# Letting a timeline-based scheduler order the instructions of a two-layer diffusion-step kernel

## The chip, the cores and the metric

The kernel runs on one core of a Trainium2 chip. The metric is the device time of one execution in microseconds (us). A core has five engines that run side by side, each working through its own list of instructions in order: PE (TensorE, matmuls), DVE (VectorE), ACT (ScalarE), POOL (GpSimd) and SP (SyncE, which here only starts DMA transfers). Engines wait for each other by semaphores. So the time depends not only on what is computed but also on the order in which each engine's list is written.

## The reference

One inference step of a hybrid backbone with two layers, on 128 prompt tokens and 512 latent tokens. Both go through the same weights, each modulated by its own condition. Layer 0 mixes tokens by latent attention (MLA) and neighbourhood attention, layer 1 by grouped-query attention. Each is followed by a SwiGLU feed-forward network (FFN), and a final norm ends the step. Cut to what matters here:

```python
def swiglu(h, w_in, w_out):
    gate, up = jnp.split(h @ w_in, 2, axis=-1)
    return (jax.nn.silu(gate) * up) @ w_out
...
    for l in range(DEPTH):
        ...
        xs = xs + g1_s * out_s
        hp = modulate(rms_norm(xp, norm_ffn[l]), sh2_p, sc2_p)
        hs = modulate(rms_norm(xs, norm_ffn[l]), sh2_s, sc2_s)
        xp = xp + g2_p * swiglu(hp, w_ffn_in[l], w_ffn_out[l])
        xs = xs + g2_s * swiglu(hs, w_ffn_in[l], w_ffn_out[l])
```

## The kernel before

**Layout.** All 640 tokens lie along the free axis, the 1024 features on the partitions in 8 tiles `xr`. The tokens are halved, so a matmul works on 128 x 128 weights and 320 tokens. Each float32 operand is split into a high part and a low remainder (`h` and `l` at the end of a name), which TensorE takes as fp32r. A product then is three matmuls per 128 x 128 tile (`mm3`, line 188): high by high, high by low, low by high. ACT makes the high part with a copy, DVE the low part with a subtraction, for weights (`unit`, line 175) and for activations (`rsplit`, line 456).

**Stages.** Input projections and attention of layer 0, output projection and residual (`mixer_out`, line 1115, tiles `oa0a` to `oa7b`, weights `oaw0` to `oaw7`), FFN (`ffn`, line 1214), then the same for layer 1 (tiles `oc`), and the final norm. Side work is mixed in: the modulation vectors of layer 1 are formed by passes on DVE over weights `wm` (tile `junk`, line 1796).

**The FFN's first half.** The 2816 hidden features are 22 blocks. Blocks 0 and 1 are done with plain products (`eight`). Blocks 2 to 21 use seven products over half the reduction and half the tokens in place of eight. Per block `n` these are: 11 (bank `fg`, weights `wX`), D (bank `fd`, `wY`), N (into `fg`, `wZ`), 21 (bank `fu`, `wX`), 22 (into `fd`, `wZ`), C (into `fg`, `wY`) and E (into `fg`, `wW`). Each is 12 matmuls. Between them banks are read out: ACT copies `fg` after product 11 to `p`, `fd` after D, `fg` after N to `u`; DVE forms `up` from `fu` and `fd`, and after C it forms `g<-fg,p`, which ACT's Silu turns into half of `sg`. E then adds into the same bank `fg` and gives the other half. In the code E of a block is issued in the loop's next pass:

```python
            after(PE.last, lambda: product(b5, w.Y, 0, "D", True))
            act(S.activation, p5, b5[:, :HT], AF.Copy)
...
                jb, jg, jW, jup, jsg = job
                product(jg, jW, 0, "E", False)
...
            product(g, w.Y, 512, "C", False)
            dve(V.tensor_tensor, g2, g[:, :HT], p5, ALU.add)
            act(S.activation, sg[:, HT:T], g2, AF.Silu, scale=-1.0)
            job, w = (fb, g, w.W, up, sg), n
```

DVE and ACT instructions of this loop go through `Line` (line 1233), which pins each behind the one before on its engine. PE's products aren't pinned there, except D. The hidden tiles are `hd` (kept) or are spilled to memory and read back as `hr`.

**The FFN's second half.** Tiles `fo` add up products of hidden tiles with weights `wo`, which are loaded, split and used one after another (`wout`). The residual (line 319) adds the result to `xr` on DVE.

**What sets the order.** The program names operations in one sequence. The framework's scheduler (`tile.TileContext`, line 2249) turns this into one list per engine, with the semaphores that data and buffers need. It may move an operation as long as its inputs, its buffers and the pins (`issue_after`, used by `after`, `run` and `Line`) allow. The pools (`bufs=`) decide how far loads can run ahead.

## Time and profile before

| | |
|---|---|
| median of 3 runs | 1482.27 us (1481.26 to 1484.97) |
| the profiled execution's own time (its span) | 1482.4 us |
| instructions in the profile | 25722 |
| read from memory, written | 192.23 MB, 34.69 MB |
| DMA transfers started by SP (queue q1) | 219.73 MB, 43.3% of 16 engines' span |

A row of the profile gives the start, the duration, the engine, the source line (L63 is PE's matmul helper, L1239 the `Line` helper, so names of tiles tell the rows apart), the operation, output and inputs, shape and count. In square brackets stands how long the engine was idle before, and what released it. Some other rows give a group's times as min/median/max ns. The names leave out the numbers of blocks and layers: `fg<-h01E,wW` is product E of any block in layer 0, `fg<-h11E,wW` of layer 1.

### The profile page before, as it was taken

How to read it: one execution, taken by the hardware profiler on the slowest of the kernel's cores; microseconds unless marked ns; L12 is line 12 of the kernel's file. 1: busy time of each engine (PE TensorE's matmuls, PEld its weight loads, DVE VectorE, ACT ScalarE, POOL GpSimd, SP SyncE). 2: the span in 40 equal slices, each digit the busy share in tenths (PEclk: the TensorE clock that was granted, in tenths of full speed). 3: DMA queues.
4: the chain of work that ended last, by engine and by line, in shares of the span. 5: the costliest groups of instructions: out<-in, count | busy, mean ns of one | idle time of the engine just before them, and what ended most of it. 6: DMA issues, size and time to landing. Idle time of an engine off the chain costs nothing.

```text
span 1482.4 us, 25722 instructions
## 1 busy us (share of the span) xinstructions
PE 1443.7 (97%) x9785; PEld 1394.3 (94%) x9785; DVE 1210.9 (82%) x2278; ACT 772.0 (52%) x1525; POOL 207.0 (14%) x298
## 2 busy tenths in 40 slices
PE   5999989999999999999999999999999999999997
PEld 4988978889999999999999999989999999999996
DVE  5786788886999999977997888775899999954496
ACT  5445677873755444441123666663755555542253
POOL 0226534432000000000001322222000000000000
PEclk9999999999999999999999999999999999999998
DMA  9644511016055555569763211004055556668522
GB/s 368 223 146 138 181 39 43 30 32 211 29 196 171 187 185 183 185 211 344 275 209 128 86 55 46 29 31 135 30 186 177 184 192 206 212 224 308 194 87 72
DMA packets 79900, 228.61 MB, mean 154 GB/s; under 512 B 8864, under 2 KB 14272, under 8 KB 79392
## 3 DMA queue, kind: packets, MB, share of 16 engines
q1 hardware_dynamic: 76832, 219.73, 43.3%
q0 software_dynamic: 1600, 5.14, 1.0%
q10 hardware_dynamic: 1344, 2.10, 0.4%
q8 instruction: 77, 1.26, 0.3%
q14 instruction: 47, 0.39, 0.1%
HBM read 192.23 MB, written 34.69 MB: 153 GB/s over the span
## 4 chain that ended last, share of the span: by engine, by line
PE 83%; DVE 7%; ACT 5%; DMA 2%; issue 2%; POOL 0%; DVEq 0%; ACTq 0%; SPq 0%; POOLq 0%
PE fg L63 21%; PE fd L63 9%; PE fo L63 8%; PE fu L63 6%; PE gq L63 3%; PE nq L63 2%; PE nk L63 2%; PE fo_2b L63 1%; PE fo_0b L63 1%; PE gs L63 1%; PE fo_2a L63 1%; PE fo_0a L63 1%; PE go L63 1%; PE mod L63 1%; PE fo_4b L63 1%
## 5 line engine op out<-in xcount | busy, mean ns | idle before, releaser
L1796 DVE SCALAR_TENSOR_TENSOR junk<-wm,cb 128x1024 bf16<-128x1024 f32 x62 | 75.6, 1220 | 4.6 <-DMA wm<-in_wm 4.1
L1239 ACT ACTIVATE sg<-g 128x320 f32<-128x320 f32 x34 | 16.0, 472 | 114.9 <-DVE g L1239 114.9
L63 PE MATMUL gq<-h10h,wgq 128*128 128x320 f32 x256 | 66.7, 318 | 0.0
L255 POOL TENSOR_SCALAR h10h<-h10t,gs,mods 128x320 fp32r<-128x320 f32 x4 | 3.6, 890 | 429.4 <-DVE h10t L249 427.7
L1239 DVE SCALAR_TENSOR_TENSOR junk<-wm,cb 128x1024 bf16<-128x1024 f32 x50 | 61.0, 1221 | 0.8
L1239 DVE TENSOR_TENSOR wY<-s,wY 128x1024 fp32r<-128x1024 f32 x40 | 48.8, 1220 | 1.1 <-ACT wY L1239 1.0
L1239 DVE TENSOR_TENSOR wZ<-s,wZ 128x1024 fp32r<-128x1024 f32 x40 | 48.8, 1220 | 0.0
L63 PEld LDWEIGHTS gq<-h10h,wgq 128*128 128x128 f32 x256 | 45.0, 188 | 0.9 <-PE gtp L67 0.2
L1239 ACT ACTIVATE wZ<-s 128x1024 fp32r<-128x1024 f32 x40 | 42.4, 1060 | 0.1
L1239 ACT ACTIVATE wY<-s 128x1024 fp32r<-128x1024 f32 x40 | 42.0, 1049 | 0.0
L63 PE MATMUL gq<-h10l,wgq 128*128 128x320 f32 x128 | 39.5, 308 | 0.0
L1978 ACT ACTIVATE gp<-gs,gb,rq 128x640 f32<-128x640 f32 (+1 forms) x40 | 31.9, 797 | 14.5 <-DVE gb L1977 14.1
L63 PE MATMUL fg<-h11E,wW 128*128 128x320 f32 x240 | 38.7, 310 | 0.0
L63 PE MATMUL fg<-h01q,wX 128*128 128x320 f32 x240 | 38.6, 309 | 0.0
L63 PE MATMUL fg<-h11q,wX 128*128 128x320 f32 x240 | 38.6, 309 | 0.0
L63 PE MATMUL fg<-h01N,wZ 128*128 128x320 f32 x240 | 38.6, 309 | 0.0
L63 PE MATMUL fg<-h11N,wZ 128*128 128x320 f32 x240 | 38.6, 309 | 0.0
L63 PE MATMUL fu<-h01q,wX 128*128 128x320 f32 x240 | 38.6, 308 | 0.0
L63 PE MATMUL fu<-h11q,wX 128*128 128x320 f32 x240 | 38.6, 309 | 0.0
L63 PE MATMUL fg<-h01E,wW 128*128 128x320 f32 x240 | 38.6, 309 | 0.0
L63 PE MATMUL fd<-h01q,wZ 128*128 128x320 f32 x240 | 38.5, 309 | 0.0
L63 PE MATMUL fd<-h11q,wZ 128*128 128x320 f32 x240 | 38.5, 309 | 0.0
(3226 smaller groups left out, 5249.6 us busy)
## 6 DMA issues: line engine op xcount, KB each, us to landing
wm<-in_wm SPq DMA_DIRECT2D x48, 512.0 KB, 3.6
mraw<-in_wm SPq DMA_DIRECT2D x8, 1024.0 KB, 15.4
mraw<-in_wm SPq DMA_DIRECT2D x16, 512.0 KB, 3.9
hr_T<-sp_T SPq DMA_DIRECT2D x21, 320.0 KB, 5.9
hr_B<-sp_B SPq DMA_DIRECT2D x18, 320.0 KB, 6.1
mrow<-in_wm0g POOLq DMA_DIRECT2D x8, 512.0 KB, 6.2
wm<-in_wm0g SPq DMA_DIRECT2D x8, 512.0 KB, 3.4
x<-in_xT SPq DMA_DIRECT2D x8, 320.0 KB, 5.7
```

The costliest lines, as they stand in the source:

```text
L63: cls.last = nc.tensor.matmul(*a, **k)
L255: G.tensor_scalar(h[:, c0:c1], t, self.gsl[:, k, 0:1], self.ml[:, self.sh + k, 0:1], ALU.mult, ALU.add)
L1239: self.last = after(self.last, lambda: op(*a, **k))
L1796: def step(kind, at, line=lambda op, *a, **k: op(*a, **k)):
L1978: weighed.append((S.activation(dst, src, AF.Exp, bias=nb, scale=rq[:, j:j + 1], accum_out=ll[:, j:j + 1]), v))
```

## The change

One argument: the scheduler no longer finds the order by its default rule but with a simulation of the engines' timelines.

```diff
     for name, shape in _OUTS:
         args.append(nc.dram_tensor(f"out_{name}", shape, F32, kind="ExternalOutput").ap())
-    with tile.TileContext(nc) as tc:
+    with tile.TileContext(nc, schedule_with_timeline_sim=True) as tc:
         body(tc, *args)
```

The instructions are the same in both kernels, engine by engine; only their order differs, and with it the semaphore waits and some buffers' turns. PE's list changes most in the FFN loops of both layers (up to 82 places), around the output projections (up to 75) and in the FFN's second half (up to 88). It is the same in the stretch from 111 to 296 us of the profile. DVE's and ACT's lists are the same inside the FFN loops and differ by small moves elsewhere. The three places that the prediction rests on follow; in them a name's last number only tells tiles of one name apart.

*PE in the FFN loop of layer 0.* `fg_8` is the bank of block 8. Before, between product C and product E of block 8 (`h01C`, `h01E`):

```order
L63 MATMUL fg_8_6073<-h01C_4787,wY_8_5934 128x320 x3
L63 MATMUL fg_8_6073<-h01C_4788,wY_8_5934 128x320 x3
L63 MATMUL fg_9_6209<-h01q_4765,wX_9_6069 128x320 x3
L63 MATMUL fg_9_6209<-h01q_4766,wX_9_6069 128x320 x3
L63 MATMUL fg_9_6209<-h01q_4767,wX_9_6069 128x320 x3
L63 MATMUL fg_9_6209<-h01q_4768,wX_9_6069 128x320 x3
L63 MATMUL fd_9_6193<-h01D_4781,wY_9_6070 128x320 x3
L63 MATMUL fd_9_6193<-h01D_4782,wY_9_6070 128x320 x3
L63 MATMUL fd_9_6193<-h01D_4783,wY_9_6070 128x320 x3
L63 MATMUL fd_9_6193<-h01D_4784,wY_9_6070 128x320 x3
L63 MATMUL fg_8_6073<-h01E_4793,wW_8_5987 128x320 x3
```

Now at the same place of PE's list:

```order
L63 MATMUL fd_9_6193<-h01D_4784,wY_9_6070 128x320 x3
L63 MATMUL fg_8_6073<-h01C_4785,wY_8_5934 128x320 x3
L63 MATMUL fg_8_6073<-h01C_4786,wY_8_5934 128x320 x3
L63 MATMUL fg_8_6073<-h01C_4787,wY_8_5934 128x320 x3
L63 MATMUL fg_8_6073<-h01C_4788,wY_8_5934 128x320 x3
L63 MATMUL fg_8_6073<-h01E_4793,wW_8_5987 128x320 x3
L63 MATMUL fg_8_6073<-h01E_4794,wW_8_5987 128x320 x3
L63 MATMUL fg_8_6073<-h01E_4795,wW_8_5987 128x320 x3
L63 MATMUL fg_8_6073<-h01E_4796,wW_8_5987 128x320 x3
L63 MATMUL fg_10_6345<-h01q_4765,wX_10_6205 128x320 x2
L63 MATMUL fu_10_6346<-h01q_4769,wX_10_6205 128x320 x2
L63 MATMUL fg_9_6209<-h01N_4789,wZ_9_6071 128x320 x3
```

Product D of block 9 and product 11 of block 9 have moved ahead of C of block 8, so E follows C with nothing between; two matmuls each of products 11 and 21 of block 10 come behind E.

*PE where the attention of layer 0 ends.* `mo` and `mpp3o` are the last attention values, `oMs3` is their split, `oa` the output projection. Now PE's list has:

```order
L63 MATMUL mo_4223<-mts_4l,mv_2867 128x512
L63 MATMUL mpp3o<-mpp3pth,mv_2851 128x128
L63 MATMUL mpp3o<-mpp3ptl,mv_2851 128x128
L63 MATMUL mpp3o<-mpp3pth,mv_2851 128x128
L63 MATMUL mpp3o<-mpp3ptl,mv_2851 128x128
L63 MATMUL oa0a<-oMs3h,oaw_3439 128x320
L63 MATMUL oa0b<-oMs3h,oaw_3439 128x320
L63 MATMUL oa1a<-oMs3h,oaw_4331 128x320
L63 MATMUL oa1b<-oMs3h,oaw_4331 128x320
L63 MATMUL oa2a<-oMs3h,oaw_4412 128x320
L63 MATMUL oa0a<-oMs3l,oaw_3439 128x320
```

Before, 45 matmuls into `oa0b`, `oa1a` and `oa1b` stood between `mpp3o` and the first `oMs3h`; they and 21 matmuls into `oa2a` have moved ahead of the last values.

*DVE behind that place.* `xr_4379` and `xr_4393` are tiles 0 and 1 of the residual, `oaw_4546` is the weight tile oaw4. Before:

```order
L1822 COPY xr_4716<-oMs3l 128x1
L323 SCALAR_TENSOR_TENSOR xr_4379<-oa0a,mods_98,xr_4379 128x320
L323 SCALAR_TENSOR_TENSOR xr_4379<-oa0b,mods_98,xr_4379 128x192
L323 SCALAR_TENSOR_TENSOR xr_4379<-oa0b,mods_98,xr_4379 128x128
L323 SCALAR_TENSOR_TENSOR xr_4393<-oa1a,mods_98,xr_4393 128x320
L323 SCALAR_TENSOR_TENSOR xr_4393<-oa1b,mods_98,xr_4393 128x192
L323 SCALAR_TENSOR_TENSOR xr_4393<-oa1b,mods_98,xr_4393 128x128
L185 TENSOR_TENSOR oaw_4546<-oaw4r,oaw_4546 128x1024
```

Now:

```order
L1822 COPY xr_4716<-oMs3l 128x1
L185 TENSOR_TENSOR oaw_4546<-oaw4r,oaw_4546 128x1024
L323 SCALAR_TENSOR_TENSOR xr_4379<-oa0a,mods_98,xr_4379 128x320
L323 SCALAR_TENSOR_TENSOR xr_4379<-oa0b,mods_98,xr_4379 128x192
L323 SCALAR_TENSOR_TENSOR xr_4379<-oa0b,mods_98,xr_4379 128x128
```

The low part of oaw4 has moved ahead of the residual of tile 0.

Where the FFN loops end, `hd_0` (the last block's hidden tile) is needed by PE six matmuls after the last product E; before, 39 output matmuls stood there. On ACT in layer 0 the split of `wo_13` has moved ahead of `hd_0h`, and on DVE three passes over `wm` stand ahead of the last `sg`. On SP the reads of spilled tiles `hr` have moved ahead of the loads `wo_45` (layer 0) and `wo_26`, `wo_36` and `wo_45` (layer 1).

## The prediction, made before the changed kernel ran

> **What bounds the kernel now.** I read the page's busy line and the engine shares of the chain of waits first: how full TensorE is decides whether an order can win or only lose.

> ```profile
> PE 1443.7 (97%) x9785; PEld 1394.3 (94%) x9785; DVE 1210.9 (82%) x2278; ACT 772.0 (52%) x1525; POOL 207.0 (14%) x298
> PE 83%; DVE 7%; ACT 5%; DMA 2%; issue 2%; POOL 0%; DVEq 0%; ACTq 0%; SPq 0%; POOLq 0%
> ```

> The profiled execution has a span of 1482.4 us and nothing around it, and the median of the runs is 1482.27, so I count from 1482.4. TensorE (PE) is not busy for 1482.4 − 1443.7 = 38.7 us. That is all that any new order could gain. Next the view by stretches of time (width, then busy us of PE, weight loads, VectorE, ScalarE and GpSimd, the granted clock, the DMA share, GB/s) shows where these holes are.

> ```profile
> 185.00:296.00 111.00, 102.97 (x641) 91.50 (x641) 96.43 (x230) 87.92 (x210) 47.77 (x67) 0.98 0.11 37
> 296.00:345.00 49.00, 47.08 (x311) 43.13 (x310) 36.48 (x77) 30.71 (x63) 14.57 (x15) 1.00 0.29 94
> 407.00:666.00 259.00, 259.00 (x1768) 258.81 (x1767) 237.79 (x353) 128.30 (x213) 0.00 (x0) 1.00 0.56 187
> 962.00:1036.00 74.00, 73.47 (x485) 69.45 (x484) 48.65 (x91) 38.44 (x76) 18.15 (x14) 1.00 0.24 78
> 1073.00:1332.00 259.00, 259.00 (x1767) 258.70 (x1766) 234.97 (x373) 138.38 (x247) 0.00 (x0) 1.00 0.58 196
> 1470.00:1482.40 12.40, 2.01 (x8) 0.87 (x6) 8.31 (x22) 3.06 (x6) 0.00 (x0) 0.62 0.60 212
> ```

> The two FFN loops (407 to 666 and 1073 to 1332) have no hole at all: an order can only open one there. The joins from attention to output projection (296 to 345, 962 to 1036) have 1.9 and 0.5 us. The attention of layer 0 (185 to 296) has 8.0, but PE's order there is unchanged.

> **The FFN loops: one wait per block is uncovered.** The timeline of PE shows the order of before within a block; the page models matmul ends, so starts are what counts.

> ```profile
> 493.53 1.92 PE L63 MATMUL fg<-h01C,wY 128*128 128x320 f32 x12
> 495.29 1.93 PE L63 MATMUL fg<-h01q,wX 128*128 128x320 f32 x12
> 497.05 1.92 PE L63 MATMUL fd<-h01D,wY 128*128 128x320 f32 x12
> 498.81 1.48 PE L63 MATMUL fg<-h01E,wW 128*128 128x320 f32 x9
> ```

> Twelve matmuls take 1.76 us (495.29 − 493.53), 0.147 each; a block has 84, 12.32 us. Product E adds into the bank that product C has filled, and may not start before VectorE's `g<-fg,p` has read it. Before, 24 other matmuls, 3.5 us, stand between C and E and cover this. In the new order E follows C directly for blocks 4 to 19 of each layer, 32 places (block 20 has 7 matmuls between, block 21 has 22). PE then stands still for the whole round trip, whose three pieces have rows where VectorE was free and waiting:

> ```profile
> 1309.70 1.92 PE L63 MATMUL fg<-h11C,wY 128*128 128x320 f32 x12
> 1311.66 0.49 DVE L1239 TENSOR_TENSOR g<-fg,p 128x320 f32<-128x320 f32 x1 [1.20 <-PE fg L63]
> L1239 DVE TENSOR_TENSOR g<-fg,p x40: 480/491/492, 426.1 to 1324.0; 128x320 f32<-128x320 f32 x40
> 1323.98 0.49 DVE L1239 TENSOR_TENSOR g<-fg,p 128x320 f32<-128x320 f32 x1 [0.64 <-PE fg L63]
> 1324.53 1.15 PE L63 MATMUL fg<-h11E,wW 128*128 128x320 f32 x6
> ```

> C's last matmul starts at 1309.70 + 11 × 0.147 = 1311.31, and g 0.35 later. g takes 0.49. In the other place g ends at 1324.47 and PE's E starts 0.06 later. Without a wait the next matmul would start 0.147 after C's last. So a place costs 0.35 + 0.49 + 0.06 − 0.15 = **0.75 us**, and the loops 32 × 0.75 = 24.0. From below the place costs at least g and the handoff, 0.55 (17.6 in all). From above I allow the hand-back to take one matmul slot longer, 0.84 (26.9).

> Is more uncovered behind it? E is followed by two matmuls of the next wX product, whose high half ScalarE makes after g:

> ```profile
> 483.98 0.48 DVE L1239 TENSOR_TENSOR g<-fg,p 128x320 f32<-128x320 f32 x1
> 496.03 0.48 DVE L1239 TENSOR_TENSOR g<-fg,p 128x320 f32<-128x320 f32 x1
> 496.54 0.47 ACT L1239 ACTIVATE sg<-g 128x320 f32<-128x320 f32 x1 [4.17 <-DVE g L1239]
> 496.92 1.04 ACT L1239 ACTIVATE wX<-wu_10r 128x1024 fp32r<-128x1024 f32 x1
> 499.08 1.22 DVE L1239 TENSOR_TENSOR wX<-wu_10r,wX 128x1024 fp32r<-128x1024 f32 x1
> ```

> The high half is ready 497.96 − 496.51 = 1.45 us after g ends, the low half 3.79 after. PE needs them after 12 matmuls (1.76 + 0.06 = 1.82) and after 28 (4.17). Both are covered, with about 0.4 to spare each. VectorE goes from one g (483.98) to the next (496.03) in 12.05 us. The new period is 12.32 + 0.75 = 13.07, so VectorE gets free time and is no bound.

> **The joins from attention to output projection.** The new order pulls 66 output matmuls ahead of the last attention values, so they no longer cover what follows.

> ```profile
> 328.74 0.50 PE L63 MATMUL mo<-mts_4l,mv 128*128 128x512 f32 x1
> 329.48 0.36 PE L63 MATMUL oa0b<-oMs2h,oaw 128*128 128x320 f32 x1
> 331.72 0.74 ACT L459 ACTIVATE oMs3h<-oM 128x640 fp32r<-128x640 f32 x1 [0.65 <-DVE oM L443]
> 332.49 0.82 DVE L460 TENSOR_TENSOR oMs3l<-oM,oMs3h 128x640 fp32r<-128x640 f32 x1 [0.80 <-ACT oMs3h L459]
> 336.13 0.31 PE L63 MATMUL oa0a<-oMs3h,oaw 128*128 128x320 f32 x1
> 337.21 1.06 ACT L184 ACTIVATE oaw<-oaw3r 128x1024 fp32r<-128x1024 f32 x1 [4.75 <-PE oa0b L63]
> 337.48 0.55 DVE L323 SCALAR_TENSOR_TENSOR xr<-oa0a,mods,xr 128x320 f32<-128x320 f32 x1 [3.55 <-DMA xr<-in_xT]
> ```

> The last matmul into mo starts at 328.74 and the four into mpp3o behind it have gone out by 329.48. From there the chain over ScalarE and VectorE gives the high half at 332.46 and the low half at 333.31. Before, PE comes to them at 336.13. Now it stands at the high half from 329.48 on: 3.0, then has five matmuls (0.73) for the 0.85 to the low half: **3.1** in all. The ends are 1.6, if the chain starts earlier against PE, and 3.1. Behind that, `oa2b` needs the bank that the residual of `oa0a` and `oa0b` sets free. That residual starts 337.48 − 333.31 = 4.2 after the low half, when its load has landed, and its pieces take 1.2 (0.55 and two more). In VectorE's new order it also stands behind the split of oaw4, and so behind two ScalarE passes of 1.06 and a VectorE pass of 1.2 (the wX row): no later than that load. PE has ten matmuls (1.5) for these 5.4: **3.9**. The residuals of the later tiles queue behind it, but PE has work ahead of those. The stretch's 1.9 us of holes get filled, 1.5 of them: 3.1 + 3.9 − 1.5 = **5.5**, with ends 1 and 7. Layer 1 has the same join, with its residual first and no oaw4 ahead of it: I take **3**, with ends 0 and 5.

> **The loop exits.** Before, the output matmuls from 658.45 to 664.17 cover the way from the last E to `hd_0`; most of them now stand ahead of E, and six are left.

> ```profile
> 658.45 0.31 PE L63 MATMUL fo_0b<-hd_2h,wo_0a 128*128 128x320 f32 x1
> 664.17 0.31 PE L63 MATMUL fo_0a<-hd_0h,wo_0a 128*128 128x320 f32 x1
> 1326.59 0.44 ACT L1239 ACTIVATE sg<-fg 128x320 f32<-128x320 f32 x1 [1.62 <-PE fg L63]
> 1327.05 1.28 ACT L159 ACT_TABLE_LOAD   x1
> 1328.34 0.74 ACT L1281 ACTIVATE hd_0h<-sg 128x640 fp32r<-128x640 f32 x1
> 662.46 0.84 ACT L1588 ACTIVATE wo<-wo_13r 128x768 fp32r<-128x768 f32 x1 [1.33 <-DMA wo_13r<-in_wFO]
> ```

> From the last E to hd_0's high half: 1329.08 − 1326.59 = 2.5, less 6 × 0.147 = 0.9 of cover: 1.6 to 1.7 in layer 1. In layer 0 the order of ScalarE puts the split of wo_13 (0.84) ahead of it: 2.5. Together **4.2**. On VectorE three passes over wm tiles that wait for loads also stand ahead of hd_0 in layer 0; if those loads are as late as wo_13r is here, up to 4 more: ends 3 and 8.

> **The rest.** SP's queue in the output stages puts spilled hidden tiles (hr) ahead of wo_45 in layer 0 and of wo_26, wo_36 and wo_45 in layer 1. Weights land some us before PE's need in my walk through the queue, so 0, with 0 and 5 as ends. At the end of the program the chain into the last norm is longer by about one to two VectorE passes of 0.5 to 1: **2**, ends 0 and 4. VectorE's and ScalarE's small swaps in attention and at the loop heads go both ways: 0, ends −4 and 4.

> Sum: 24.0 + 5.5 + 3 + 4.2 + 2 = 38.7, so 1482.4 + 38.7 = **1521**.

> **Rivals.**
> *The attention stage gains and the wait is nearly free (faster).* The small swaps in front of attention let inputs come earlier and close its 8.0 us of holes and the joins' 2.4, and E's wait costs next to nothing: 1482.4 − 10 = 1472. It decides at 10 / 32 = 0.31 us a place, below g's own 0.49; E can't be passed by other matmuls unless PE runs out of order, which no row shows. Chance 0.03. With g at its price and these holes closed the time is 1510, inside my range.
> *The change is real but hidden elsewhere (no change).* Loops at 17.6 with gains of 10 and no loss in joins and exits give 1490, still above 0.3%; only with the loops' wait at half of that, 1481, is nothing left to measure. Chance 0.03.
> *The joins, exits and loads are worse than I priced.* Their upper ends: 7 + 5 + 8 + 5 + 4 = 29 with the loops at 24 give 1535. For it: each stall ends on a chain through ScalarE, VectorE and a load; against it: the loads start earlier as well. Chance 0.12.
> *The clock falls.* If holes make the clock fall, the loops run slower throughout.

> ```profile
> 200.00:210.00 10.00, 7.87 (x39) 6.81 (x39) 8.22 (x29) 6.29 (x18) 2.21 (x5) 0.83 0.04 14
> 250.00:260.00 10.00, 9.11 (x60) 7.94 (x59) 9.21 (x20) 7.16 (x17) 4.53 (x7) 1.00 0.15 55
> ```

> A stretch with 2.1 of 10 us idle has 0.83; one with 0.9 idle has 1.00. The loops would be idle for 0.75 of 13.07, less than the second. At 0.83 they would lose 32 × 12.32 × 0.2 = 79 us: about 1600. Chance 0.02. [...]

> **How the numbers follow.** My forecast has 0.80 (1508 to 1532), the worse joins 0.12, the clock 0.02, no change 0.03, faster 0.03. 0.3%, 4.4 us, is about what a measurement here tells from no change. The low end is loops at 17.6 with small joins and exits (1 + 0 + 3): 1504. The high end is the worse rival with the loops at 26.9: 1538. Faster 0.03, same 0.03, slower 0.94.

> **What would show it.** In the loops PE's idle time before `fg<-E`, released by VectorE's g, should be about 0.6 us a place, 32 times, with a period near 13.07 and PE no longer full in 407 to 700. If that wait is missing, the main term is wrong. If idle time stands before wX or wZ products, ScalarE's or VectorE's chain was tighter than I worked out. The joins should show holes before `oa0a<-oMs3h` and `oa2b`, the exits before `fo_0a<-hd_0h`, on ScalarE or VectorE; a DMA as releaser there would speak for the worse case. A granted clock below 1.00 in the loops would speak for the last rival.

## The result, and the profile after

| | before | after |
|---|---|---|
| median | 1482.8 us (1481.3 to 1485.0) | 1542.3 us (1540.3 to 1544.6) |
| profiled execution (span) | 1482.4 us | 1541.1 us |
| ratio to before, 95% interval | | 1.040 (1.039 to 1.041) |

The changed kernel is slower by 4.0%, 59.5 us in the medians and 58.7 us between the two profiled executions. The forecast was 1521, with 1538 as the upper end of its range: the direction and the main term held, and some 20 us are missing from the sum.

The page of the changed kernel, busy times and engine shares of the chain of waits:

```profile
PE 1460.3 (95%) x9785; PEld 1400.2 (91%) x9785; DVE 1206.2 (78%) x2278; ACT 766.2 (50%) x1525; POOL 213.1 (14%) x298
...
PE 74%; DVE 14%; ACT 6%; DMA 4%; issue 2%; SPq 0%; DVEq 0%; ACTq 0%
```

PE now stands still for 1541.1 − 1460.3 = 80.8 us instead of 38.7. It is also busy for 16.6 us longer with the same 9785 matmuls. Part of this is slower matmuls, as shown below; part is the page's way of counting: a matmul ahead of a hole counts as busy for 0.31 us, where in an unbroken row the next one starts after 0.147. The share of VectorE (DVE) in the chain has doubled from 7% to 14%. The view of waits of the changed kernel names PE's new ones (sum in us, times, longest):

```profile
PE fg L63 <- DVE g L1239: 18.7, 32, 0.6
...
PE oa2b L63 <- DVE xr L323: 4.9, 1, 4.9
...
PE fo_0a L63 <- ACT hd_0h L1281: 4.9, 2, 3.9
PE gs L63 <- ACT gp L1978: 4.8, 4, 2.9
PE fn1p L63 <- DVE fn1acc L215: 3.3, 1, 3.3
...
PE oa0a L63 <- ACT oMs3h L459: 2.9, 1, 2.9
...
PE oc0a L63 <- ACT oGs7h L459: 1.3, 1, 1.3
PE fg L63 <- ACT wZ L1239: 1.3, 2, 0.7
PE fo L63 <- ACT sg L1239: 1.1, 2, 0.5
```

And the view by stretches of time, with the columns of the prediction (the granted clock stands behind POOL's busy time):

```profile
335.00:352.00 17.00, 9.22 (x46) 8.63 (x45) 8.93 (x23) 6.04 (x10) 2.35 (x1) 0.80 0.73 258
400.00:443.00 43.00, 41.30 (x273) 39.78 (x272) 38.11 (x76) 29.30 (x64) 0.00 (x0) 1.00 0.40 137
443.00:684.00 241.00, 231.67 (x1553) 227.45 (x1552) 211.33 (x307) 110.53 (x185) 0.00 (x0) 1.00 0.54 174
684.00:697.00 13.00, 8.52 (x44) 8.00 (x43) 7.19 (x11) 3.74 (x5) 0.00 (x0) 0.74 0.99 349
697.00:797.00 100.00, 99.87 (x681) 99.52 (x679) 80.18 (x143) 19.51 (x28) 0.00 (x0) 1.00 0.72 242
1005.00:1021.00 16.00, 12.86 (x72) 11.97 (x71) 11.84 (x23) 9.44 (x20) 4.97 (x4) 0.79 0.10 35
```

The loop (443 to 684), full before, is idle for 9.3 us at clock 1.00. The loop's head (400 to 443) is idle for 1.7, where the kernel before had none in the matching stretch:

```profile
393.00:434.00 41.00, 41.00 (x281) 40.89 (x280) 37.70 (x72) 26.99 (x56) 0.00 (x0) 1.00 0.41 144
```

At the join (335), the exit (684) and the end of layer 1's attention (1005) holes come with a clock of 0.74 to 0.80: the matmuls that follow are slower too (0.27 us from one start to the next, not 0.147).

How far the changed kernel is behind at the same matmul of both traces gives the loss by stage. At the last E the same work is compared: before, PE has done it only with the 33 output matmuls that now stand ahead of E. All lags come from one execution of each kernel, and two executions with the same lists can differ by some 2 us (at 45 us the run with N moved, below, is 2.0 us behind the changed kernel).

| matmul | before, us | after, us | behind | the stage that ends here |
|---|---|---|---|---|
| `mo6<-mts6_2l` | 318.0 | 314.5 | −3.5 | inputs and attention of layer 0: −3.5 (2.8 of it from 191 us on) |
| `oa2b<-oMs2h` | 344.0 | 351.6 | 7.6 | join of layer 0: +11.1 |
| `fg_3<-h01q3` | 395.0 | 401.2 | 6.3 | output projection and norm: −1.3 |
| last C of block 3 | 433.5 | 442.9 | 9.4 | loop head: +3.1 |
| last E of block 21 (before: with 33 output matmuls behind it) | 663.1 | 686.1 | 22.9 | loop: +13.5 |
| first `fo_0a<-hr` | 668.0 | 697.8 | 29.9 | exit: +7.0 |
| `gq70` | 962.0 | 994.7 | 32.7 | FFN's second half: +0.6 (30.5 behind at 798.3); attention of layer 1: +2.2 |
| `oc0a<-oGs4h` | 984.2 | 1022.1 | 37.9 | end of that attention: +5.2 |
| last C of block 3 | 1101.6 | 1142.7 | 41.0 | join: +0.8 (38.7 behind at 1045.1); head: +2.3 |
| last E of block 21 (before: the same) | 1331.7 | 1386.1 | 54.4 | loop: +13.4 |
| first `fo_0a<-hd_0h` | 1332.7 | 1389.0 | 56.3 | exit: +1.9 |
| end | 1482.4 | 1541.1 | 58.7 | second half, last norm: +2.4 |

One place of the loop, from the timeline of the changed kernel (PE and DVE):

```profile
577.35 1.92 PE L63 MATMUL fg<-h01C,wY 128*128 128x320 f32 x12
...
579.31 0.49 DVE L1239 TENSOR_TENSOR g<-fg,p 128x320 f32<-128x320 f32 x1 [1.02 <-PE fg L63]
579.86 2.03 PE L63 MATMUL fg<-h01E,wW 128*128 128x320 f32 x12 [0.58 <-DVE g L1239]
...
581.72 0.45 PE L63 MATMUL fg<-h01q,wX 128*128 128x320 f32 x2
```

C's last matmul starts at 577.35 + 11 × 0.147 = 578.97 and E's first 0.89 later, 0.74 more than a slot. VectorE is waiting for C, so the chain is the forecast's. But E's twelve matmuls take 581.72 − 579.86 = 1.86 instead of 1.76: the second comes 0.10 late. So a place costs 0.845, the 32 places 27.0, and a block takes 13.17 us (the next C starts at 590.52), where 13.07 was forecast.

The join of layer 0 (PE, GpSimd, DVE):

```profile
341.50 0.31 PE L63 MATMUL oa2a<-oMs3h,oaw 128*128 128x320 f32 x1
...
342.11 2.35 POOL L185 TENSOR_TENSOR oaw<-oaw3r,oaw 128x1024 fp32r<-128x1024 f32 x1 [20.16 <-ACT oaw L184]
...
343.01 2.53 DVE L185 TENSOR_TENSOR oaw<-oaw4r,oaw 128x1024 fp32r<-128x1024 f32 x1 [2.37 <-ACT oaw L184]
345.46 0.54 DVE L323 SCALAR_TENSOR_TENSOR xr<-oa0a,mods,xr 128x320 f32<-128x320 f32 x1
...
346.73 0.60 PE L63 MATMUL oa2b<-oNs0h,oaw 128*128 128x320 f32 x1 [4.92 <-DVE xr L323]
```

The residual stands behind the low part of oaw4, as the order lists said, and that pass takes 2.53 us, not 1.2.

The exit of layer 0 (DVE, ACT, PE):

```profile
686.65 1.23 DVE L1796 SCALAR_TENSOR_TENSOR junk<-wm,cb 128x1024 bf16<-128x1024 f32 x1 [3.19 <-DMA wm<-in_wm]
...
690.34 0.82 DVE L1239 TENSOR_TENSOR sg<-up,sg 128x640 f32<-128x640 f32 x1
...
691.20 0.74 ACT L1281 ACTIVATE hd_0h<-sg 128x640 fp32r<-128x640 f32 x1 [0.71 <-DMA hr_7h<-sp_7h]
...
691.98 0.64 PE L63 MATMUL fo_0a<-hd_0h,wo_0a 128*128 128x320 f32 x1 [3.95 <-ACT hd_0h L1281]
```

Three wm passes hold the last sg back until 690.34. hd_0h starts right when sg ends (691.16); the DMA that the row names as releaser isn't what it waited for.

A hole that the prediction did not see, at the end of layer 1's attention (DVE, ACT, PE):

```profile
1009.94 0.82 DVE L1967 TENSOR_REDUCE gn<-gs 128x1 f32<-128x640 f32 x1
...
1013.14 0.15 DVE L1977 TENSOR_TENSOR gb<-gn,rq 128x1 f32<-128x1 f32 x1
...
1013.38 0.89 ACT L1978 ACTIVATE gp<-gs,gb,rq 128x640 f32<-128x640 f32 x1 [1.24 <-DVE gb L1977]
...
1014.41 0.90 PE L63 MATMUL gs<-gkh,gqh 128*128 128x320 f32 x2 [2.89 <-ACT gp L1978]
```

The row maximum `gn` is done at 1010.76, but the short `gb` after it stands behind other splits until 1013.14. ScalarE's exponential and PE's bank wait for it. The join of layer 1 has a hole as well: the first matmul on the last attention values waits for ScalarE's split of them (the row `PE oc0a L63 <- ACT oGs7h`), as in layer 0.

### The profile page after: what moved, and what is told of

It is laid out like the page before. It is cut to its first block, busy times and chain, and to the rows that moved or that the text cites. A ratio compares the mean times of both kernels' runs of the same rounds, so it can differ in the third digit from the quotient of the medians.

```text
span 1541.1 us, 25787 instructions
## 1 busy us (share of the span) xinstructions
PE 1460.3 (95%) x9785; PEld 1400.2 (91%) x9785; DVE 1206.2 (78%) x2278; ACT 766.2 (50%) x1525; POOL 213.1 (14%) x298
## 4 chain that ended last, share of the span: by engine, by line
PE 74%; DVE 14%; ACT 6%; DMA 4%; issue 2%; SPq 0%; DVEq 0%; ACTq 0%
PE fg L63 17%; PE fd L63 8%; PE fo L63 5%; PE fu L63 4%; PE gq L63 2%; PE nk L63 2%; PE nq L63 2%; PE gs L63 1%; PE go L63 1%; PE ms L63 1%; PE mod L63 1%; DVE g L1239 1%; PE fo_0b L63 1%; PE fo_2b L63 1%; DVE junk L1796 1%
## 5 line engine op out<-in xcount | busy, mean ns | idle before, releaser
L1239 ACT ACTIVATE sg<-g 128x320 f32<-128x320 f32 x34 | 16.0, 471 | 149.9 <-DVE g L1239 149.9
L63 PE MATMUL gq<-h10h,wgq 128*128 128x320 f32 x256 | 66.7, 317 | 0.0
L1239 DVE SCALAR_TENSOR_TENSOR junk<-wm,cb 128x1024 bf16<-128x1024 f32 x50 | 61.0, 1220 | 0.8
L1239 DVE TENSOR_TENSOR g<-fg,p 128x320 f32<-128x320 f32 x40 | 19.6, 490 | 40.2 <-PE fg L63 40.2
L1239 DVE TENSOR_TENSOR wY<-s,wY 128x1024 fp32r<-128x1024 f32 x40 | 48.7, 1218 | 0.9 <-ACT wY L1239 0.9
L63 PE MATMUL fg<-h01E,wW 128*128 128x320 f32 x240 | 40.1, 316 | 9.3 <-DVE g L1239 9.3
L63 PE MATMUL fg<-h11E,wW 128*128 128x320 f32 x240 | 40.1, 316 | 9.3 <-DVE g L1239 9.3
L1239 DVE TENSOR_TENSOR wZ<-s,wZ 128x1024 fp32r<-128x1024 f32 x40 | 48.7, 1218 | 0.0
L63 PEld LDWEIGHTS fg<-h01E,wW 128*128 128x128 f32 x240 | 35.4, 188 | 13.5 <-DVE g L1239 13.5
L63 PEld LDWEIGHTS fg<-h11E,wW 128*128 128x128 f32 x240 | 35.4, 188 | 13.5 <-DVE g L1239 13.5
L63 PEld LDWEIGHTS gq<-h10h,wgq 128*128 128x128 f32 x256 | 45.0, 189 | 0.7
L1239 ACT ACTIVATE wZ<-s 128x1024 fp32r<-128x1024 f32 x40 | 42.4, 1061 | 2.9 <-DVE s L1239 2.0
L1239 ACT ACTIVATE wY<-s 128x1024 fp32r<-128x1024 f32 x40 | 42.0, 1050 | 1.2 <-DVE s L1239 1.2
L63 PE MATMUL fu<-h01q,wX 128*128 128x320 f32 x240 | 41.9, 309 | 0.0
L63 PE MATMUL fu<-h11q,wX 128*128 128x320 f32 x240 | 41.9, 309 | 0.0
L63 PE MATMUL fg<-h11q,wX 128*128 128x320 f32 x240 | 41.5, 309 | 0.0
L63 PE MATMUL fg<-h01q,wX 128*128 128x320 f32 x240 | 41.5, 309 | 0.0
L63 PE MATMUL fg<-h01N,wZ 128*128 128x320 f32 x240 | 39.0, 309 | 0.7 <-ACT wZ L1239 0.7
L63 PE MATMUL fg<-h11N,wZ 128*128 128x320 f32 x240 | 39.0, 309 | 0.7 <-ACT wZ L1239 0.7
L63 PE MATMUL gq<-h10l,wgq 128*128 128x320 f32 x128 | 39.4, 308 | 0.0
```

The costliest lines, as they stand in the source:

```text
L63: cls.last = nc.tensor.matmul(*a, **k)
L1239: self.last = after(self.last, lambda: op(*a, **k))
```

## The experiments

In all of them each engine's list is written out in full and pinned, instruction behind instruction, so that nothing but the named moves differs from the kernel that the run starts from. The pin adds no wait; up to the first moved product the run with E moved away stays within 0.4 us of the changed kernel's times:

```diff
         body(tc, *args)
+        _in_order(nc, tc)
...
+        if last is not None:
+            tc.add_manual_dep(i, last, mybir.DependencyInfo(mybir.DependencyClass.NoSync, mybir.DependencyReason.DATA), reason="order")
+        last = i.name
```

Theory: the time goes where PE's holes stand (E's wait in the loops, heads, joins, exits), each made by the order on the engine that it waits for, plus slow matmuls behind long holes. Rivals: one cause behind it all (loads or traffic), or holes that only show what would be late anyway.

### Can E's wait be covered by moving one product?

**E moved away from C** (changed kernel, blocks 4 to 19, both layers):

```diff
 fg_4<-h01C,wY_4 x12
-fg_4<-h01E,wW_4 x12
 fg_6<-h01q,wX_6 x2
 fu_6<-h01q,wX_6 x2
 fg_5<-h01N,wZ_5 x12
+fg_4<-h01E,wW_4 x12
```

> The changed kernel with every engine's order kept, except that product E of blocks 4 to 19 in both layers stands 16 matmuls behind C (two each of the next products 11 and 21, then product N) instead of directly behind it. Theory: each of the 32 places costs 0.746 us of waiting and 0.10 for E's first matmul, whose successor comes late, as the changed kernel's trace shows: 32 x 0.845 = 27.0, so 1542.3 - 27.0 = 1515. Rival: the wait only covers that ScalarE's and VectorE's weights (wZ above all, now needed 12 matmuls sooner) are no earlier; then the idle time moves to N or to the wX products, and the time stays above 1527.

Measured: 1610.6 us, ratio 1.086 (1.085 to 1.088), 68 us more than the changed kernel: the rival's side, and far beyond it. PE stands 2.2 us at each of the 32 places.

**N moved between C and E**, wX behind E:

```diff
 fg_4<-h01C,wY_4 x12
+fg_5<-h01N,wZ_5 x12
 fg_4<-h01E,wW_4 x12
 fg_6<-h01q,wX_6 x2
 fu_6<-h01q,wX_6 x2
-fg_5<-h01N,wZ_5 x12
```

> The changed kernel with every order kept, except that product N of the next block is moved between C and E of blocks 4 to 19 in both layers (twelve matmuls, 1.76 us, for the 0.85 us that E waits); the first wX matmuls stay behind E. Theory: now the wX matmuls come 3.6 us after C, later than ScalarE's high half (2.3 us after C, by 0.35 + 0.49 + 1.45), so the wait of 0.746 and the 0.10 behind it go at all 32 places: 1542.3 - 27.0 = 1515. Rival: another operand is late again, as wX was where E alone was moved away; the time stays above 1527.

Measured: 1632.7 us, ratio 1.102 (1.100 to 1.103). The rival again, with 2.5 us at each place. The view of waits of the first run, then of the second:

```profile
PE fg L63 <- ACT wX L1239: 65.3, 32, 2.1
```
```profile
PE fg L63 <- ACT p L1239: 75.7, 32, 2.4
```

The timeline of ScalarE in the second run:

```profile
573.50 0.47 ACT L1239 ACTIVATE sg<-g 128x320 f32<-128x320 f32 x1 [6.92 <-DVE g L1239]
573.87 1.04 ACT L1239 ACTIVATE wX<-wu_13r 128x1024 fp32r<-128x1024 f32 x1
574.82 0.42 ACT L1239 ACTIVATE p<-fg 128x320 f32<-128x320 f32 x1
```

ScalarE's list is fixed by hand: behind the Silu of g come the high half of wX and the read-out `p` of the next block's `fg`. So whatever PE finds behind C, be it E, wX or N, waits for something that stands behind g. With D and product 11 of the next block pulled ahead of C, E's wait is the shortest of the three. So in the changed order neither move brings the cover back, because PE runs ahead of a list that does not. The next run changes E's place alone.

**E directly behind C in the kernel before**, everything else as before:

```diff
 fg_8<-h01C,wY_8 x12
+fg_8<-h01E,wW_8 x12
 fg_9<-h01q,wX_9 x12
 fd_9<-h01D,wY_9 x12
-fg_8<-h01E,wW_8 x12
```

> The kernel before with every order kept, except that product E of blocks 4 to 19 in both layers is moved from behind D of the next block to directly behind its own C. Theory: the adjacency of C and E alone makes the loops' loss, whatever order the other products stand in: 32 x 0.845 = 27.0, so 1482.8 + 27.0 = 1510. Rival: the loss needs the new loop's other moves too (D and 11 of the next block ahead of C); then under 1500.

Measured: 1527.1 us, ratio 1.030 (1.028 to 1.031): 44.8 us of loss, not 27.0. The adjacency alone does lose time, but not at that price. Its timeline (PE and DVE):

```profile
526.26 1.92 PE L63 MATMUL fg<-h01C,wY 128*128 128x320 f32 x12
...
527.15 1.22 DVE L1239 SCALAR_TENSOR_TENSOR junk<-wm,cb 128x1024 bf16<-128x1024 f32 x1
...
528.30 0.48 DVE L1239 TENSOR_TENSOR up<-fd,u 128x320 f32<-128x320 f32 x1
528.71 0.48 DVE L1239 TENSOR_TENSOR g<-fg,p 128x320 f32<-128x320 f32 x1
...
529.24 2.03 PE L63 MATMUL fg<-h01E,wW 128*128 128x320 f32 x12 [1.06 <-DVE g L1239]
```

C's last matmul starts at 527.87 and g could start 0.35 later, but VectorE comes to it at 528.71, behind a wm pass and `up`. In the changed kernel D, moved ahead of C, gives VectorE 1.76 us to get rid of these; this is read from the rows, no run tests it alone. So the price of 0.845 holds only where VectorE stands waiting for g; in the order of before the same adjacency costs about 1.32 at most places of layer 0 (1.22 and the 0.10), and between 0.85 and 2.0 in layer 1.

### The holes at joins and exits

**Three queues on VectorE and ScalarE** (changed kernel, PE's list untouched). Of layer 0's exit, DVE:

```diff
+sg_21<-up_21,sg_21
+hd_0l<-sg_21,hd_0h
 junk19<-wm_9
 junk19<-wm_9
 junk110<-wm_10
-sg_21<-up_21,sg_21
 junk110<-wm_10
 wo_13<-wo_13r,wo_13
-hd_0l<-sg_21,hd_0h
```

> The changed kernel with PE's, GpSimd's and SyncE's order kept. On VectorE and ScalarE three places get the order of before: the residual of tiles 0 and 1 ahead of the low part of oaw4; in layer 1 the row maximum and exponential of gs7_0 ahead of splits and of ocw2; in layer 0 the last sg and hd_0 ahead of the three wm passes and of the split of wo_13. Theory: these queues make PE's three holes of 5.08, 3.06 and 4.11 us, and each of these holes, being over 3 us, is followed by about 2 us lost to half-rate matmuls. Then the holes shrink to about 2.8, 0 and 1.1, which is 8.3, and the slow stretches go, 6.3: 1542.3 - 14.6 = 1528. Rival A: PE's own order makes the holes, and the time stays within 2 us of 1542. Rival B: the slow stretches don't depend on the holes' length: 1534.

Measured: 1536.4 us, ratio 1.036 (1.035 to 1.038). The three holes shrank from 5.08, 3.06 and 4.11 us to 3.08, 0 and 1.07, as expected, and behind the last two no slow matmuls followed; behind the first they stayed (2.3 us). But only 5.9 of the 14.6 us were gained. Between 717 and 783 us 4.6 were given back. The stretch of the FFN's second half in this run, and ScalarE and PE in its timeline:

```profile
692.00:792.00 100.00, 96.80 (x651) 95.12 (x651) 78.69 (x142) 16.88 (x24) 0.00 (x0) 1.00 0.76 254
```
```profile
756.73 0.95 ACT L1588 ACTIVATE wo<-wo_10r 128x896 fp32r<-128x896 f32 x1 [9.05 <-DMA wo_10r<-in_wFO]
...
757.73 0.41 PE L63 MATMUL fo<-hr_6h,wo 128*128 128x320 f32 x1 [0.83 <-ACT wo L1588]
```

ScalarE waits 9 us for a weight load, and PE for ScalarE. In the changed kernel the matching stretch (697 to 797) is full, 99.87 of 100 us, because PE comes later. The theory's holes were right; a second limit lay behind one of them.

**The second half of layer 0 as well** (DVE, ACT and SP as before there; this line of SP shows the kind of move):

```diff
+wo_45r<-in_wFO
+wo_50r<-in_wFO
 hr_10h<-sp_10h
 hr_10l<-sp_10l
...
-wo_50r<-in_wFO
...
-wo_45r<-in_wFO
```

> The changed kernel with PE's and GpSimd's order kept; the moves of the run of the three queues, and further VectorE's, ScalarE's and SyncE's orders of before in the whole second half of layer 0's FFN (wm passes, splits and loads of wo, reads of hr). That run gave back 4.6 us there between 717 and 783 us, with PE waiting 1.1 and 0.5 us a tile for the split of wo_10, wo_20 and wo_30, loaded late. Theory: the new order of SyncE's loads and VectorE's wm passes is a second limit, hidden in the changed kernel by the exit's hole: 1536.4 - 4.6 - 1.9 (lost there already in the changed kernel) = 1530. Rival: PE's order or the traffic itself is the limit: 1536.

Measured: 1530.3 us, ratio 1.033 (1.031 to 1.034), where 1530 was expected. PE in that stretch of the run:

```profile
697.00:797.00 100.00, 100.00 (x685) 100.00 (x684) 89.47 (x164) 19.02 (x29) 0.00 (x0) 1.00 0.81 275
```

Full again, and with a larger DMA share (0.81), so the traffic itself is not the limit. It was the order of SP's loads and of VectorE's and ScalarE's passes there; which of the three counts, the run does not separate. That the time came out at 1530 is in part luck: between the two traces the second half gives 5.5 us, of which 0.6 was lost already in the changed kernel, and a wait of 1.3 us has come in ahead of the exit.

### The loop heads

**The order of before at both heads**; on PE in layer 0, for instance:

```diff
+fd_3<-h01D,wY_3 x12
+fg_3<-h01N,wZ_3 x1
+fg_2<-h01E,wW_2 x12
+fg_3<-h01N,wZ_3 x11
-fd_3<-h01D,wY_3 x2
-fg_3<-h01N,wZ_3 x2
-fd_3<-h01D,wY_3 x10
-fg_3<-h01N,wZ_3 x10
-fg_2<-h01E,wW_2 x12
 fd_3<-h01q,wZ_3 x12
```

> The changed kernel with the order of before on PE, VectorE and ScalarE from about 370 to 440 us (the norm ahead of the FFN and the first blocks of the loop) in layer 0 and at the same place in layer 1, and the load of cb ahead of two writes. Theory: the five holes of 0.3 to 0.8 us there, 2.5 a layer, and what stands beside them come from the new order, 5.8 in both layers: 1536.5. Rival: they come from loads that arrive late because the stages ahead have changed: 1542.

Measured: 1538.2 us, ratio 1.037 (1.036 to 1.039), 4.1 us less in the medians. Between the profiled executions it is 5.6 us (1541.1 to 1535.5), of which 2.2 lie in each head with the norm ahead of it and the rest in stages with the same lists. So the heads' loss does come from the new order, at some 4.1 to 4.5 us rather than 5.8.

### What a hole costs beyond itself

**28 added waits in the kernel before**, by edges that do wait:

```diff
+    for a, b in _HOLDS:
+        tc.add_manual_dep(by[a], b, mybir.DependencyInfo(mybir.DependencyClass.Sync, mybir.DependencyReason.DATA), reason="hold")
```

> The kernel before with every order kept and 28 added waits in the FFN loops (blocks 5 to 18 of both layers): E of a block, or product 11 of the next, also waits for a VectorE pass over the weights two blocks ahead, so that PE stands still for 1.0 to 5.9 us at each place, some 72 us in all. It measures what a standstill costs beyond itself. Theory A (half-rate matmuls follow only where PE stood for about 3.4 us): the 7 places of 3.3 us and more lose about 2 us each, the others nothing: 1482.4 + 72 + 14 = 1568. Theory B (PE's work is looked at in fixed spans of about 3.4 us, and a span that is idle for the larger part halves the rate: so in the run with E moved alone, where of 32 equal standstills of 2.2 us 16 were followed by 1.6 us of loss and 16 by none, in alternation): no loss at 1.0 to 1.3, at 2.0 to 2.3 in about half, at 2.7 and more in nearly all: some 17 places by 1.8, 1585. Theory C (no such loss): 1554.

Measured: one time, 1580.1 us. The 28 holes add up to 70.6 us. 14 of them were followed by slow matmuls, 27.1 us in all; behind the other 14 only the second matmul came 0.10 late. By length: none of 6 at 1.0 to 1.1 us, 5 of 10 at 1.95 to 2.25, 3 of 6 at 2.67 to 2.85, 6 of 6 at 3.28 to 5.88. Two holes of the same length in this run, in PE's timeline:

```profile
568.17 2.02 PE L63 MATMUL fg<-h01q,wX 128*128 128x320 f32 x12 [2.51 <-DVE s L1239]
...
646.89 2.44 PE L63 MATMUL fg<-h01q,wX 128*128 128x320 f32 x12 [2.51 <-DVE s L1239]
```

The twelve matmuls behind the second hole take 0.42 us longer. So it is not the length alone, and theory A falls (8 places under 3 us lost).

The granted clock that the traces record decides for fixed spans. It is 1.00 or 0.50, and in each of the 14 traces, that of the run with N moved included, it changes only at whole multiples of 3.413 us from one common start. The spans around these two holes:

```profile
563.00:566.41 3.41, 2.66 (x19) 2.40 (x17) 3.25 (x8) 0.19 (x1) 0.00 (x0) 1.00 0.87 303
566.41:569.82 3.41, 1.65 (x11) 1.66 (x12) 3.34 (x5) 1.23 (x2) 0.00 (x0) 1.00 0.38 139
569.82:573.24 3.42, 3.42 (x25) 3.42 (x24) 1.75 (x3) 2.66 (x4) 0.00 (x0) 1.00 0.45 153
644.92:648.33 3.41, 1.44 (x9) 1.44 (x10) 3.34 (x5) 1.42 (x2) 0.00 (x0) 1.00 0.39 144
648.33:651.74 3.41, 3.41 (x15) 3.41 (x14) 1.33 (x2) 2.33 (x3) 0.00 (x0) 0.50 0.48 154
```

The first hole is shared by two spans that are idle for 0.75 and 1.76 us, and the next one has 25 matmuls at 1.00. The second lies in one span, idle for 1.97, and the next has 15 at 0.50. Over the 14 traces, from 300 us on, a span at 1.00 was followed by one at 0.50 whenever PE was idle for more than 1.84 us of it by the page's busy times, and never when it was idle for less than 1.76 (84 spans at 1.00 were followed by one at 0.50, 4825 were not). So theory B is right in kind, with the limit at a little over half a span; at 2.7 us only half of the holes lost, where it expected nearly all, because a hole can be shared by two spans.

The other runs agree. In the run with E moved away, 16 of 32 holes of 2.2 us lost 1.6 us each, mostly every second one: two periods of that loop are 30.76 us, 9.01 × 3.413, so one period is 4.5 spans. In the run with N moved, 23 of 32 holes of 2.5 us lost as much. Where the spans lie relative to the kernel differs from execution to execution: around the second hole of layer 0's join, with the same lists, the clock was at 0.50 for 6.8 us in the changed kernel and for 10.2 in the run with N moved.

### Putting the rest back

**PE's order in both loops and exits**, on top of the second half put back:

```diff
+fg_8<-h01C,wY_8 x12
+fg_9<-h01q,wX_9 x12
 fd_9<-h01D,wY_9 x12
-fg_8<-h01C,wY_8 x12
 fg_8<-h01E,wW_8 x12
```

> The run with the second half of layer 0 put back (1530.3 us), and further PE's order of before in both FFN loops with their exits (all of E, C, D and the products 11, and the output matmuls around the last E), with the order of the few VectorE and ScalarE steps at the loops' ends that go with it. Theory: the 32 places lose 0.845 each, 27.0; the two waits of 0.69 behind the last E and the two of 1.07 for hd_0 go as well, 3.5: 1530.3 - 30.5 = 1499.8. Rival: PE running ahead with D and 11 had gained something elsewhere, which is lost now, or VectorE (busy 238 of 259 us before) becomes the bound: above 1505.

Measured: 1499.8 us, ratio 1.011 (1.010 to 1.013), as expected. **And the heads**, with the edit shown there:

> The same, and further the order of before at both loop heads, as in the run of the heads alone. Theory: terms of stages that lie apart add up: that run gained 5.6 from one profiled execution to the other, 2.5 of holes a layer, so 1499.8 - 5.6 = 1494.2. Rival: with the loops put back the heads' holes are covered or move: 1499.8.

Measured: 1494.7 us, ratio 1.008 (1.006 to 1.010). The terms add up. What this trace is still behind the kernel before, 10.1 us (1492.5 and 1482.4), lies in the join of layer 0 (5.0, net of the lead ahead of it), the attention of layer 1 (2.2), the join of layer 1 (0.8) and the end.

**The new order only up to the join of layer 0** (all engines up to 314 us of the profile before; from there the order of before). Against the changed kernel, on PE at the border:

```diff
-oa0a<-oMs0h,oaw0 x1
 mo6<-mts6_3h,mv3 x1
-oa0a<-oMs0l,oaw0 x1
-oa0a<-oMs0h,oaw0 x1
 mt7_0<-ident,mp7_0 x1
...
 mo6<-mts6_4h,mv4 x1
+oa0a<-oMs0h,oaw0 x1
+oa0a<-oMs0l,oaw0 x1
```

> The new order on every engine up to the last attention stage of layer 0 (314 us of the profile before), and the order of before from there on. Theory: every loss comes from the part behind, and PE was 3.4 us ahead at that point: 1482.4 - 3.4 = 1479, faster by 0.2%. Rival: the lead is lost in the join, where PE then waits for loads that are no earlier: 1482.4.

Measured: 1479.9 us, ratio 0.9984 (0.9975 to 0.9992), a gain of 2.4 us over the kernel before where 3.4 was expected, with this busy line:

```profile
PE 1441.1 (98%) x9785; PEld 1394.0 (94%) x9785; DVE 1207.1 (82%) x2278; ACT 769.6 (52%) x1525; POOL 215.6 (15%) x298
```

So most of the lead up to the join is real, and this version is faster than both kernels, than the one before by only 0.16%. **The new order through the join** on top of it (the lines marked − above come back, and the moves shown with the change as its second and third place):

> The run that is faster than the kernel before (new order up to 314 us of the profile before, 1479.9 us), with the new order carried on through the join of layer 0, up to the matmul oa2b and the residual behind it. Theory: the join loses what the changed kernel's trace has between these points, from 4.3 ahead to 7.3 behind, slow matmuls included: 1479.9 + 11.6 = 1491.5. Rival: its holes come from the later stages' loads being pulled ahead, which are as before here: under 1484.

Measured: 1491.5 us, ratio 1.005 (1.004 to 1.007), as expected: the join's holes need nothing from later stages. The exact match is partly luck, since the second hole is 4.5 us here and not 5.1, and the clock stays at 0.50 for 13.7 us and not 6.8. **The new order at the end** on top of the faster version, from the last E of layer 1 on:

> The run that is faster than the kernel before, with the new order in the second half of layer 1's FFN and the last norm (from the end of layer 1's loop on, all engines). Theory: it loses what the changed kernel loses from 56.3 behind at the first hd_0 to 58.7 at the end: 1479.9 + 2.4 = 1482.3. Rival: as in layer 0 the changed kernel's earlier losses hide a limit of the loads there, which now shows: above 1485.

Measured: 1482.9 us, ratio 1.000 (0.999 to 1.001), 3.0 us above that version, close to the expected 2.4.

## Why the prediction was right in direction and too low in size

| step | forecast | measured | where it shows |
|---|---|---|---|
| FFN loops | 24.0 (17.6 to 26.9) | 26.9 | both loops; the run with the loops put back |
| join of layer 0, with the lead before it | 5.5 (1 to 7), lead 0 | −3.5 + 11.1 = 7.6 | the run with the join alone: 11.6 |
| loop heads, with projection and norm ahead | 0 | −1.3 + 3.1 + 2.3 = 4.1 | the run of the heads: 4.1 to 4.5 |
| exits | 4.2 (3 to 8) | 7.0 + 1.9 = 8.9 | waits on `hd_0h` and `sg`, clock 0.74 |
| second half of layer 0, DMA order | 0 (0 to 5) | 0.6 | lag at 798.3 |
| attention of layer 1 | 0 | 2.2 | lag; no run undoes it alone |
| end of that attention, join of layer 1 | 3 (0 to 5) | 5.2 + 0.8 = 6.0 | waits on `gp` and `oGs7h`, clock 0.79 |
| end of program | 2 (0 to 4) | 2.4 | the run of the end: 3.0 |
| sum | 38.7 | 58.7 | |

**The loops** were right in mechanism: PE waits at 32 places for g, by VectorE, with the three pieces 0.35, 0.49 and 0.06, and the granted clock stays at 1.00. The size was off by the 0.10 that E's second matmul comes late. That its upper end, 0.84, is the same figure is luck: it stands there for a hand-back "one matmul slot longer", which would be 0.75 + 0.147 = 0.90, and the hand-back was as forecast.

**The slow matmuls** are the step that failed most. The prediction weighed a fall of the clock as a matter of the loops, all or nothing, and its sum has no term for one at the joins and exits. In fact three holes were followed by matmuls at half the clock (0.50 for 6.83 us each, from 344.70, 689.45 and 1013.71 us): the lag grows from 5.3 to 7.6 behind `oa2b`, from 27.8 to 29.9 behind `fo_0a`, and by 2.5 behind `gs`. That is some 6.9 us, spread over the rows of the joins and exits, and without it the time would lie inside the stated range. The exits would stand at 6.9, and the end of layer 1's attention with its join at 3.5, close to its 3.

**The loop heads** are the second such step: "VectorE's and ScalarE's small swaps in attention and at the loop heads go both ways: 0". Together they stayed within the stated ends of −4 and 4: −3.5 up to the end of layer 0's attention, +2.2 in layer 1's, +4.1 at the heads. But the 0 had no row behind it. At the heads, PE's own new order counts too, and before, PE was busy without a break there, as in the loops, so an order could only lose.

**The join of layer 0**: 3.1 for the first hole came out as 3.03. The second was 3.9 and is 5.08, because the pass over oaw4 took 2.53 us beside GpSimd's split of oaw3. The 1.5 credited for holes filled does not show: between the two matmuls the lag grows by 11.1, of which the two holes are 8.1 and the slow matmuls 2.3.

**The exits**: in layer 1 the hole is 1.07 instead of 1.7, in layer 0 4.11 instead of 2.5. The reason that the prediction gave for its upper end, the wm passes on VectorE ahead of hd_0, was the one that decided; it had taken the split of wo_13 instead. Not seen at all: 0.69 in each layer, where the output matmuls behind E wait for a bank that ScalarE must read first (the row `PE fo L63 <- ACT sg`).

**Layer 1**: the join has the hole of layer 0's kind, ahead of `oc0a<-oGs7h`, 1.3 us in the view of waits. But most of the loss lies one step earlier, at `gs7_2`, where the short `gb` stands behind splits on VectorE.

**The end**: of the 2.4, half is lost already in layer 1's second half, where PE waits 0.9 us for ScalarE's split of `wo_2S`. The other half is the chain named: VectorE's scaling of `lead` stands 2.13 us waiting for ScalarE ahead of the last residual, which then reaches the norm late.

```profile
1529.23 0.49 DVE L2098 TENSOR_TENSOR lead<-lead,fn1rs 128x320 f32<-128x320 f32 x1 [2.13 <-ACT fn1rs L223]
```

Of the rivals, "the joins, exits and loads are worse" came nearest (1535). It had the loops at 24, no heads and no slow matmuls. The starting point, "nothing around" the span of 1482.4, is not quite so: an execution takes 1.8 us longer than its span (1542.9 and 1541.1 for the changed kernel). It shifts nothing, as the median before is 1482.8.

## What to carry to other kernels

Where one engine is busy without a break, price every stretch in which its list changes, not only the one with the largest visible move; a new order can only open holes there. When one engine's order is freed and the others' lists are pinned by hand, the freed one runs ahead of them. Here the wait could then not be covered by moving a single product: the next product waited for something that the pinned list held back too. Undo such changes a stage at a time: a hole that goes may uncover a later limit, as in layer 0's second half, and a version with the new order only up to the first join was faster than both.
